# Which products of a decoder block begin with a matmul whose columns go in blocks

## The chip, the core and the metric

The kernel runs on one core of one Trainium2 chip. The metric is device time in microseconds (us) of one execution of the whole program. Weights and activations are float32 in HBM; most matmuls take them as float32r, the form in which TensorE multiplies a float32 operand.

## What is computed

One layer of a hybrid decoder trunk on 512 tokens of width 1024, with a memory of 256 tokens. Cut to what matters here:

```python
h = rmsnorm(x) * g
proj = h @ w_in                       # 9216 columns: B, C, v | u, ug | q | three gates
y_a = (B * conv3(C * v)) @ w_a_out
u   = conv31(u * sigmoid(ug)) + bias
y_b = silu(layernorm(u)) @ w_b_out
k, vm = split(rmsnorm(mem) @ w_kv)
s   = (q @ k.T) / 16                  # 4 heads of 256, 256 memory tokens
y_c = (softmax(s) @ vm) @ w_att_out
x   = x + (g0 * y_a + g1 * y_b + g2 * y_c) @ w_o
h2  = rmsnorm(x) * g2
gt, up = split(conv3(h2 @ w_up))      # 2 x 2816 columns
x   = x + (silu(gt) * up) @ w_down
out = rmsnorm(x) * g3
```

## The kernel before

**Products in three parts.** A float32 operand is split into a high part (rounded to float32r) and a low part (the rest). A product then takes three matmuls: high by high, high by low, low by high. ScalarE writes the high part of a weight unit (`whi`, line 665), VectorE the low part (`wlo`, line 669). A unit has 128 x 1024 elements; there are four pairs of such buffers, so unit n+4 waits until TensorE is done with unit n.

**Quads.** The wide projections (`w_in`, `w_up`, and `w_b_out`) are done in quads: two column groups of 256 by two halves of the depth by two halves of the tokens, with seven block products instead of eight, numbered 1 to 7. Sums of weight blocks are formed by DMAs that add (issued by GpSimd, line 790), sums of activations once by VectorE. A quad product, for instance `(("up", 1), 4)`, is one call of `multiply`: 2 x 4 x 3 = 24 matmuls of 128 x 128 weights by 256 columns, all recorded at line 845. The stationary operand is the weight part, the moving operand a form of the activations (`ft4h` is the high part of form t4). Results add up in PSUM banks (`bank`); ScalarE copies and VectorE adds them out (jobs `r1` to `r7`).

**The other products.** `product` (lines 616 to 618) makes three matmuls of a stationary activation by moving weights or keys: values `V`, scores `s`, the weighted values `o`, the output projection `wo`, and the down projection `pd`. The `merge` products are at lines 1654 to 1656. Of these, scores have 256 columns and the last group of `pd` (key `g`) partly so; the others have 512. The scores of a head are two calls with 12 matmuls each (`("s", h, 0)` and `("s", h, 1)`); after the softmax, its probabilities are transposed by four 128 x 128 transposes a call (`("pt", h, 0)`, `("pt", h, 1)`, line 1350).

**A matmul in blocks.** In some products the first matmul alone reads its moving columns, and writes its PSUM columns, in another order: the columns are cut into runs of `run` elements, first all even runs, then all odd ones. Column and place stay together, so the result is the same. It is done by a view:

```python
t.rearrange("p (b two r) -> p two b r", two=2, r=run)
```

Before the change the first matmul of a quad product has runs of 16 where the product just before it in TensorE's order has long rows (`V`, `o`, `merge`, `pd`, most of `wo`) or is a mean or a sum of squares; in the up projection, number 7 of quads 3 to 10 has runs of 64, 16 or 8 in turn. Each call of `scores` begins with a matmul in runs of 16 too.

**Order.** TensorE's order is written out: `seq`, a list of keys put together by loops over the quads and then changed by the pairs in `MOVES` (a key, and the key that it is put ahead of). A planner then places the work of ScalarE, VectorE, SyncE and GpSimd by costs and due times, and every engine issues in the order so found. The form of a matmul's columns is in no cost, so it moves nothing in any of these orders.

Of the kernel before, what the change touches and what calls it, by code (L numbers as in the profile page):

```python
# [58 lines left out]
WO_WHOLE = "f"  # L59
# [87 lines left out]
}  # L147

MOVES = [
    (("v", "squares"), (("gate", 1, 1), 6)),  # L150
    (("v", "rows"), ("merge", 0, 3, 0)),
# [341 lines left out]
def hybrid_block_kernel(  # L493
# [19 lines left out]
    nc = tc.nc  # L513
# [31 lines left out]
    def make(key, dtype=F32):  # L545

        ring, i = jobs.place[key]
        label = "_".join(str(k) for k in key) if isinstance(key, tuple) else key
        if ring == "ps":
            t = psum.tile([P, SEQ], F32, tag=f"ps{i}", name=name(str(key[0])))  # L550
        elif ring == "wf":
            t = wts.tile([P, 1024], F32, tag=f"wf{i}", name=name("wf"), bufs=1)
        else:
            t = places[ring].tile([P, 1024], dtype, tag=f"{ring}{i}", name=name(str(key[0])))
        tiles[key] = t
        return t

    def two(key):

        return tiles[key].rearrange("p (c n) -> p c n", c=2)  # L560
# [4 lines left out]
    def halves(key):  # L565

        return tiles[key].rearrange("p (c n) -> p c n", c=2)
# [32 lines left out]
    def par(key, i):  # L600
        return pk[:, cols[key] + i : cols[key] + i + 1]
# [4 lines left out]
    nc.scalar.dma_start(out=pk[:, :N_GAINS], in_=packed[:, :N_GAINS])  # L606
    nc.scalar.copy(mean_w, mean_col.broadcast_to([P, P]))

    def in_blocks(t, run):
        return t.rearrange("p (b two r) -> p two b r", two=2, r=run)  # L610

    def product(ps, w_hi, w_lo, s_hi, s_lo, start, stop, again=False, run=None):


        to, col = (ps, w_hi) if run is None else (in_blocks(ps, run), in_blocks(w_hi, run))
        nc.tensor.matmul(to, s_hi, col, start=start, stop=False, skip_group_check=again)  # L616
        nc.tensor.matmul(ps, s_hi, w_lo, start=False, stop=False, skip_group_check=again)  # L617
        nc.tensor.matmul(ps, s_lo, w_hi, start=False, stop=stop, skip_group_check=again)  # L618

# [7 lines left out]
    seq, pe_jobs, unit_uses, unit_at = [], {}, [], {}  # L627
# [192 lines left out]

    def long_rows(key):

        return key[0] in ("V", "o", "merge", "pd") or key[0] == "wo" and key[1] not in WO_WHOLE or key[1] in ("mean", "squares")

    def multiply(q, f, act):
        if f in (1, 2, 5):
            make(("bank", q, BANK_OF[f]))
        ps = halves(("bank", q, BANK_OF[f]))
        (w_hi, w_lo), (hi, lo) = w_units.pop((q, f)), form[act, OPERAND[f]]
        run = None  # L830
        if long_rows(seq[seq.index((q, f)) - 1]):
            run = 16
        elif q[0] == "up" and f == 7 and q[1] > 2:
            run = (64, 16, 8)[q[1] % 3]

        for c in range(2):
            at = slice(c * P, (c + 1) * P)
            for k in range(4):
                first = f in (1, 2, 5) and k == 0 and c == 0
                again = not (f in (1, 2, 5) and c == 0)  # L840
                for n, (w, a) in enumerate(((w_hi, hi), (w_hi, lo), (w_lo, hi))):
                    to, col = ps[:, c, :], a[k]
                    if run is not None and (c, k, n) == (0, 0, 0):
                        to, col = in_blocks(to, run), in_blocks(col, run)
                    nc.tensor.matmul(  # L845
                        to, w[:, k, at], col, start=first and n == 0,
                        stop=k == 3 and n == 2, skip_group_check=again,
                    )

    def multiply_job(q, f, act, unit=True):  # L850
        bank = ("bank", q, BANK_OF[f])
        after = [("wl", (q, f))]
        if (act, OPERAND[f]) in form_ready:
            after += form_ready[act, OPERAND[f]]
        else:
            after.append(("fl", act, OPERAND[f]))
        after += {6: [("r1", q)], 7: [("r6", q)], 4: [("r7", q)], 3: [("r5", q)]}.get(f, [])
        pe((q, f), 24 * MM_QUAD, lambda: multiply(q, f, act), after,
           take=[(bank, "ps")] if f in (1, 2, 5) else [], use=[] if f in (1, 2, 5) else [bank],
           unit=unit)  # L860
# [252 lines left out]
    def values_product(hp, kp, i):  # L1113
        w_hi, w_lo = w_units["V", hp, kp]
        first = kp == 0 and i == 0
        for c in range(MC):
            bank = ("bank", "V", hp, c)
            ps = make(bank) if first else tiles[bank]
            at, k = slice(c * P, (c + 1) * P), 2 * (kp % 2) + i
            product(  # L1120
                ps, w_hi[:, i, :], w_lo[:, i, :], tiles["mh", kp // 2][:, k, at],
                tiles["ml", kp // 2][:, k, at], first, kp == 3 and i == 1,
            )
# [101 lines left out]
    for i in range(2):  # L1225
        a, b = 2 * i, 2 * i + 1
# [106 lines left out]
    def scores(h, tp):  # L1333
        make(("bank", "s", h, tp))
        ps = halves(("bank", "s", h, tp))
        k = tiles["k", h].rearrange("p (s c n) -> p s c n", s=2, c=2)
        for i in range(2):
            t = 2 * tp + i
            at = slice(t * P, (t + 1) * P)
            for c in range(2):  # L1340
                product(
                    ps[:, i, :], k[:, 0, c, :], k[:, 1, c, :], two(("qh", h))[:, c, at],
                    two(("ql", h))[:, c, at], c == 0 and i == 0, c == 1, again=i > 0,
                    run=16 if (i, c) == (0, 0) else None,
                )

    def transposed(h, c):
# [6 lines left out]
    def weighted(h, d):  # L1354
        ps = make(("bank", "o", h, d))
        at = slice(h % 2 * 256 + d * P, h % 2 * 256 + (d + 1) * P)
        for c in range(MC):
            v_hi, v_lo = (two((s, h // 2))[:, c, at] for s in ("vh", "vl"))
            product(
                ps, two(("pth", h))[:, c, :], two(("ptl", h))[:, c, :], v_hi, v_lo,  # L1360
                c == 0, c == MC - 1,
            )

    def pe_scores(h):
        for tp in range(2):
            pe(("s", h, tp), 12 * MM_HALF, lambda tp=tp: scores(h, tp), [("kl", h), ("ql", h)],
               take=[(("bank", "s", h, tp), "ps")], use=[("k", h), ("qh", h), ("ql", h)],
               unit=False)
# [253 lines left out]
    for p in range(4):  # L1622
# [5 lines left out]
            lambda k, j, p=p: par("conv_a_w", k * KC + 2 * p + j), [("CV", p), ("ldp",)], ANY,  # L1628
# [40 lines left out]
    for br in (2, 0, 1):  # L1669
        for m in range(4):  # L1670
# [3 lines left out]
            gate = ("g", br, m)  # L1674
# [304 lines left out]
    for t in range(NT):  # L1979
# [8 lines left out]
        for i in range(2):  # L1988
            bank, r = ("bank", "tr", t, i), t // 2
# [37 lines left out]
    for q in range(QUADS):  # L2027
        up = ("up", q)
# [4 lines left out]
        for value, src, acc in ((0, ("gt", q), ("gtc", q)), (1, ("uu", q), ("upc", q))):  # L2033
            conv3_jobs(
                ("cf", q, value), src, acc,
                lambda k, j, q=q, v=value: par(
                    "conv_ffn_w", k * 2 * FC + v * FC + 2 * q + j),
# [253 lines left out]
    for u, ps in enumerate(PAIR_UNITS):  # L2291
        n = ps.stop - ps.start
        for p in "abe":
            i, j = {"a": (0, 0), "b": (1, 0), "e": (1, 1)}[p]
# [167 lines left out]

    for key, other in MOVES:
        seq.remove(key)
# [70 lines left out]
```

## Time and profile before

| what | us |
|---|---|
| median of 3 runs | 922.1 (920.11, 922.1, 924.8) |
| the profiled execution's own time | 922.01 |
| its span, first to last instruction | 920.2 |
| outside of the span | 1.8 |
| TensorE busy | 909.2 (99%) |
| VectorE busy | 849.7 (92%) |
| ScalarE busy | 685.9 (75%) |
| mean granted clock of TensorE | 0.998 |

A matmul's recorded duration (276 ns at line 845) is longer than the distance between two of them, since they overlap in the pipeline. What a matmul costs in a running stream is read from the distance of two starts, or from how many there are in a stretch. Weight loads (PEld) run beside the matmuls.

### The profile page before, as it was taken

What the parts mean: (1) busy time and instruction counts of PE and PEld (TensorE: products, weight loads), DVE (VectorE), ACT (ScalarE), POOL (GpSimd) and SP (SyncE); (2) the same over time, 40 slices, a digit from 0 to 9 for tenths busy, and PEclk for the clock granted to TensorE, in tenths of its full rate; (3) what the DMA queues carried; (4) which work ended last, traced back from release to release, by engine and by line L of the source; (5) the groups of instructions that cost most, each with busy time, mean ns of one, the idle gap of its engine ahead of it and who ended that gap; (6) DMA issues with size and microseconds to landing.
All of it is one profiled execution on the core that took longest, in us unless ns stands there. A gap on an engine that the chain in (4) does not pass through costs nothing.

```text
span 920.2 us, 17065 instructions
## 1 busy us (share of the span) xinstructions
PE 909.2 (99%) x6797; PEld 859.1 (93%) x6797; DVE 849.7 (92%) x969; ACT 685.9 (75%) x940; POOL 137.1 (15%) x164
## 2 busy tenths in 40 slices
PE   8999999999999999999999999999999999999997
PEld 8999999999989999999899997899999999988886
DVE  6997999999999998999888989898979899999977
ACT  8767989889997785979658964776667677765556
POOL 0021111100110221110111211121211121002300
PEclk9999999999999999999999999999999999999999
DMA  9999689564887999884969999999999698779972
GB/s 366 371 286 205 135 183 205 138 136 118 196 188 212 212 192 236 207 181 123 235 128 249 210 264 334 233 233 311 251 222 217 154 190 177 198 240 322 267 139 92
DMA packets 55520, 196.91 MB, mean 214 GB/s; under 512 B 6288, under 2 KB 6416, under 8 KB 55440
## 3 DMA queue, kind: packets, MB, share of 16 engines
q0 software_dynamic: 22608, 81.54, 49.3%
q1 hardware_dynamic: 32544, 114.02, 34.4%
q8 instruction: 53, 0.87, 0.4%
q10 hardware_dynamic: 288, 0.27, 0.1%
q14 instruction: 27, 0.22, 0.1%
HBM read 191.60 MB, written 4.19 MB: 213 GB/s over the span
## 4 chain that ended last, share of the span: by engine, by line
PE 91%; DVE 5%; DMA 2%; issue 1%; ACT 0%; SPq 0%; DVEq 0%; ACTq 0%
PE bank L845 61%; PE bank L618 6%; PE bank L616 6%; PE bank L617 6%; PE bank L1655 3%; PE bank L1656 3%; PE bank L1654 3%; DVE wlo L669 2%; PE bank L1107 1%; DMA wf<-in_w_v 1%; DMA ('up', 3)_967_7394<-in_w_up 1%; PE bank L1888 1%; DVE gtc L1610 1%; DVE zl L2224 0%; DMA wf<-in_w_kv 0%
## 5 line engine op out<-in xcount | busy, mean ns | idle before, releaser
L665 ACT CAST whi<-wf 128x1024 fp32r<-128x1024 f32 x200 | 208.1, 1045 | 86.2 <-PE bank L845 52.3
L669 DVE TENSOR_TENSOR wlo<-wf,whi 128x1024 fp32r<-128x1024 f32 x194 | 233.1, 1211 | 13.3 <-ACT whi L665 13.0
L1422 ACT ACTIVATE tp<-u,pk 128x511 f32<-128x511 f32 (+22 forms) x184 | 118.6, 703 | 2.3 <-DVE acc L1429 2.3
L1429 DVE TENSOR_TENSOR acc<-acc,tp 128x1022 f32<-128x1022 f32 (+22 forms) x92 | 109.1, 1188 | 6.5 <-ACT tp L1422 4.9
L790 POOL DMA_DIRECT2D wf<-in_w_in x46 | 41.6, 934 | 238.7 <-DVE wlo L669 216.4
L845 PE MATMUL bank<-ft4h,whi 128*128 128x256 f32 x248 | 68.7, 277 | 1.0 <-DVE uu L622 1.0
L845 PE MATMUL bank<-ft7h,whi 128*128 128x256 f32 x248 | 68.8, 277 | 0.7 <-ACT gt L887 0.7
L845 PE MATMUL bank<-fb11h,whi 128*128 128x256 f32 x248 | 68.8, 277 | 0.0
L845 PE MATMUL bank<-fb10h,whi 128*128 128x256 f32 x248 | 68.7, 277 | 0.0
L845 PE MATMUL bank<-ft6h,whi 128*128 128x256 f32 x248 | 68.7, 277 | 0.0
L845 PE MATMUL bank<-fb00l,whi 128*128 128x256 f32 x248 | 68.7, 277 | 0.0
L845 PE MATMUL bank<-fb00h,whi 128*128 128x256 f32 x248 | 68.7, 277 | 0.0
L845 PE MATMUL bank<-ft6l,whi 128*128 128x256 f32 x248 | 68.6, 277 | 0.0
L845 PE MATMUL bank<-ft4l,whi 128*128 128x256 f32 x248 | 68.6, 277 | 0.0
L845 PE MATMUL bank<-ft5h,whi 128*128 128x256 f32 x248 | 68.6, 277 | 0.0
L845 PE MATMUL bank<-ft4h,wlo 128*128 128x256 f32 x248 | 68.6, 277 | 0.0
L845 PE MATMUL bank<-ft7l,whi 128*128 128x256 f32 x248 | 68.6, 277 | 0.0
L845 PE MATMUL bank<-ft6h,wlo 128*128 128x256 f32 x248 | 68.6, 277 | 0.0
L845 PE MATMUL bank<-ft5l,whi 128*128 128x256 f32 x248 | 68.6, 277 | 0.0
L845 PE MATMUL bank<-fb11l,whi 128*128 128x256 f32 x248 | 68.6, 277 | 0.0
L845 PE MATMUL bank<-ft5h,wlo 128*128 128x256 f32 x248 | 68.6, 277 | 0.0
L845 PE MATMUL bank<-fb11h,wlo 128*128 128x256 f32 x248 | 68.6, 277 | 0.0
(413 smaller groups left out, 3168.5 us busy)
## 6 DMA issues: line engine op xcount, KB each, us to landing
wf<-in_w_in SPq DMA_DIRECT2D x50, 512.0 KB, 5.1
wf<-in_w_in POOLq DMA_DIRECT2D x46, 512.0 KB, 6.5
wf<-in_w_up POOLq DMA_DIRECT2D x33, 512.0 KB, 6.9
wf<-in_w_up SPq DMA_DIRECT2D x30, 512.0 KB, 6.5
wf<-in_w_down SPq DMA_DIRECT2D x15, 512.0 KB, 4.6
wf<-in_w_kv SPq DMA_DIRECT2D x8, 512.0 KB, 8.9
wf<-in_w_v SPq DMA_DIRECT2D x8, 512.0 KB, 8.1
wf<-in_w_att_out SPq DMA_DIRECT2D x8, 512.0 KB, 4.7
```

The source lines that it names most:

```text
L616: nc.tensor.matmul(to, s_hi, col, start=start, stop=False, skip_group_check=again)
L617: nc.tensor.matmul(ps, s_hi, w_lo, start=False, stop=False, skip_group_check=again)
L618: nc.tensor.matmul(ps, s_lo, w_hi, start=False, stop=stop, skip_group_check=again)
L665: nc.scalar.copy(parts[0], src())
L669: nc.vector.tensor_tensor(lo, src(), hi.bitcast(F32), op=ALU.subtract)
L790: nc.gpsimd.dma_start(out=tiles[key], in_=block(w, col[c], k), accum_op=ALU.add)
L845: nc.tensor.matmul(to, w[:, k, at], col, start=first and n == 0, stop=k == 3 and n == 2, skip_group_check=again,)
L1422: nc.scalar.activation(two(("tp", p, s))[:, j, s:], two(("u", p))[:, j, : SEQ - s], AF.Copy, scale=weight(j),)
L1429: nc.vector.tensor_tensor(a, a, two(("tp", p, s))[:, :, s:], op=ALU.add)
L1654: nc.tensor.matmul(ps, w_hi[:, i, at], hi, start=first, stop=False)
L1655: nc.tensor.matmul(ps, w_hi[:, i, at], lo, start=False, stop=False)
L1656: nc.tensor.matmul(ps, w_lo[:, i, at], hi, start=False, stop=last)
```

## The change

A set `FRESH` names nine quad products. A quad product now begins with a matmul in runs of 16 if it is in `FRESH`, or follows a transpose of probabilities (`pt`), beside the cases that there were. Five quad products follow a `pt`: `(("gate",2,0),2)`, `(("q",1),3)`, `(("gate",2,0),6)`, `(("gate",2,1),2)` and `(("gate",2,0),3)`. The scores lose their matmul in blocks: `product` no longer has a parameter for it. No instruction is added or taken away; what differs is the order of columns in the first matmul of 14 quad products and of the eight calls of `scores`.

```diff
+FRESH = {
+    (("glu", 1), 3), (("q", 1), 5), (("cv", 0), 1), (("cv", 2), 1), (("cv", 2), 2), (("bb", 1), 6),
+    (("gate", 0, 0), 3), (("up", 0), 7), (("up", 1), 4),
+}
...
-    def in_blocks(t, run):
-        return t.rearrange("p (b two r) -> p two b r", two=2, r=run)
-
-    def product(ps, w_hi, w_lo, s_hi, s_lo, start, stop, again=False, run=None):
-        to, col = (ps, w_hi) if run is None else (in_blocks(ps, run), in_blocks(w_hi, run))
-        nc.tensor.matmul(to, s_hi, col, start=start, stop=False, skip_group_check=again)
+    def product(ps, w_hi, w_lo, s_hi, s_lo, start, stop, again=False):
+        nc.tensor.matmul(ps, s_hi, w_hi, start=start, stop=False, skip_group_check=again)
         nc.tensor.matmul(ps, s_hi, w_lo, start=False, stop=False, skip_group_check=again)
         nc.tensor.matmul(ps, s_lo, w_hi, start=False, stop=stop, skip_group_check=again)
...
-        return key[0] in ("V", "o", "merge", "pd") or key[0] == "wo" and key[1] not in WO_WHOLE or key[1] in ("mean", "squares")
+        return key[0] in ("V", "o", "merge", "pd") or key[0] == "wo" and key[1] not in WO_WHOLE or key[1] in ("mean", "squares") or key[0] == "pt"
...
-        if long_rows(seq[seq.index((q, f)) - 1]):
+        if long_rows(seq[seq.index((q, f)) - 1]) or (q, f) in FRESH:
             run = 16
...
-                        to, col = in_blocks(to, run), in_blocks(col, run)
+                        to, col = blocks(to), blocks(col)
...
                     two(("ql", h))[:, c, at], c == 0 and i == 0, c == 1, again=i > 0,
-                    run=16 if (i, c) == (0, 0) else None,
                 )
```

More of the change, by code (lines that the diff above doesn't have):

```diff
@@ L834, in multiply, with blocks @@
             run = (64, 16, 8)[q[1] % 3]
+        def blocks(t):
+            return t.rearrange("p (b two r) -> p two b r", two=2, r=run)
         for c in range(2):
```

## The prediction

> **What bounds the kernel now.** I read the page first, for its chain of work that ended last, and then the chain in order of time.
>
> ```profile
> span 920.2 us, 17065 instructions
> ...
> PE 91%; DVE 5%; DMA 2%; issue 1%; ACT 0%; SPq 0%; DVEq 0%; ACTq 0%
> ```
>
> TensorE makes 91% of the chain. So the time is mostly the number of matmuls times the distance between two of them, and a change that only reorders columns inside a matmul can act through that distance alone. The chain in order of time shows how even the distance is.
>
> ```profile
> 177.89 2.73 PE bank L845 x24
> 180.62 0.44 PE bank L1350 x4
> 181.06 2.83 PE bank L845 x24
> ...
> 210.10 2.83 PE bank L845 x24
> ...
> 290.12 146.90 PE bank L845 x1296
> ...
> 636.99 151.73 PE bank L845 x1320
> 788.76 0.50 DVE wlo L669
> ...
> 827.87 0.50 PE bank L618
> ```
>
> Columns are start, us, and what. Between 290 and 437 us 1296 quad matmuls take 146.90 us: 0.1134 us each, 2.72 us for a quad of 24. The same rate would bring 1320 of them through in 149.6 us, yet the piece from 636.99 takes 151.73, so 2.1 us too long, with no wait in it. Two single quads that follow transposes (181.06 and 210.10) show the same on a small scale: 2.83 us against 2.73 for their neighbour at 177.89. To find where the 2.1 us lie I asked for stretches, with line 845 alone.
>
> ```profile
> 640.00:680.00 40.00, 40.00 (x342) 40.00 (x341) 1.00 1.04 260
> 690.00:700.00 10.00, 10.00 (x91) 10.00 (x90) 1.00 1.00 272
> 700.00:740.00 40.00, 40.00 (x355) 40.00 (x354) 1.00 0.79 162
> ```
>
> Columns: the stretch and its length, matmul busy time and count, weight loads likewise, granted clock, DMA share, GB/s. A matmul is recorded for 0.28 us, so a stretch of 40 us counts those that started in 40.28 us: 40.28/342 = 0.1178 us against 40.28/355 = 0.1135. Busy time is full and the clock is 1.00 in both. So TensorE has two rates for the same work, 4% apart, and a train of quads keeps one for tens of us. Where the slow train begins and ends stands in the timeline.
>
> ```profile
> 636.99 0.35 PE L845 MATMUL bank<-ft4h,whi 128*128 128x256 f32 x1 [0.99 <-DVE uu L622]
> ```
>
> ```profile
> 683.00 0.28 PE L845 MATMUL bank<-ft4h,whi 128*128 128x256 f32 x1
> ...
> 685.12 0.28 PE L845 MATMUL bank<-ft7h,whi 128*128 128x256 f32 x1
> 685.24 0.28 PE L845 MATMUL bank<-ft7l,whi 128*128 128x256 f32 x1
> 685.36 0.28 PE L845 MATMUL bank<-ft7h,wlo 128*128 128x256 f32 x1
> 685.48 0.28 PE L845 MATMUL bank<-ft7h,whi 128*128 128x256 f32 x1
> ```
>
> It begins at 636.99, with the first matmul after a wait for VectorE; by the written order that is `(("up",1),4)`. It ends at 685.12, which is `(("up",4),7)`, the first quad after it that has a matmul in runs of 16: from 683.00 to 685.12 lie 18 distances of 0.1178, then three of 0.12, and from there on the quads run at 0.1134. The block in runs of 64 in `(("up",3),7)`, in the middle of that train, ended nothing. I read this as a phase of the pipeline: a wait or a transpose can leave TensorE in the slow one, it stays there as long as equal matmuls follow, and a matmul in runs of 16 throws it into the fast one.
>
> **The change, part by part.** *The guard at `(("up",1),4)`.* From 636.99 to 685.12 are 17 quads. The 16 after the first would run at 0.1134 instead of 0.1178: 16 x 24 x 0.0044 = 1.70 us. In the first quad itself, 21 distances gain 0.0044 (0.09 us) and the block costs 0.03 us, as priced next: 0.06 us won.
>
> *The eight other named quads.* Here the block goes into a train that is fast already in this execution, or, at `(("up",0),7)`, follows a wait after which the train was fast by itself. The nearest row is `(("up",7),7)`, which has runs of 16 and enters from a fast train.
>
> ```profile
> 744.99 0.28 PE L845 MATMUL bank<-ft7h,whi 128*128 128x256 f32 x1
> ...
> 747.74 0.28 PE L845 MATMUL bank<-fb00h,whi 128*128 128x256 f32 x1
> ```
>
> Its 24 matmuls take 2.75 us instead of 2.72: 0.03 us. Eight of them cost 0.24 us; the bounds are 0 and 0.3.
>
> *The five quads behind transposes.* The two slow ones (2.83) come to 2.73: 0.20 us won. The other three pay up to 0.03 each; I take 0.05. Together 0.15 us won.
>
> A rule speaks against all three. The Trainium skill (SBUF — State Buffer, section Door 1: The DMA port swizzle) says that a PSUM access pattern that is not contiguous slows matmuls significantly. If that meant a matmul of twice the time (an estimate of mine, for the page has no figure), six more blocked matmuls than before would cost 0.7 us and the sum below would be 921.0; the rows at 685.12, with distances of 0.12, speak against it for runs of 16.
>
> *The scores without a block.* All their 96 matmuls now have rows of 256 columns in plain order.
>
> ```profile
> 165.65 0.28 PE L616 MATMUL bank<-k,qh 128*128 128x256 f32 x1
> ...
> 168.51 0.29 PE L845 MATMUL bank<-fb00h,whi 128*128 128x256 f32 x1
> ```
>
> ```profile
> 911.25 0.28 PE L616 MATMUL bank<-whi,zh 128*128 128x256 f32 x1
> ...
> 913.64 0.28 PE L618 MATMUL bank<-whi,zl 128*128 128x256 f32 x1
> ```
>
> With the block, the 24 matmuls of a head take 2.86 us: 0.119 each, neither of the two rates of the quads. The nearest rows without it are the last of the down projection, made by the same helper with 256 columns: 20 distances in 2.39 us, 0.1195 each. At that price the scores stay as they are (+0.05 us for four heads); if they took the rate of the quads, 96 x 0.006 = 0.6 us would be won. I take 0, since those rows are the same helper and width. The five quads right behind scores have no block, before or after, and lie in fast trains now; if plain scores left them slow, 5 x 0.1 = 0.5 us would be lost. I take 0 here too.
>
> *Does the end move with TensorE?* The chain above leaves TensorE at 788.76 and runs over VectorE until 827.87, where TensorE takes over to the end. So the 1.70 us count only if VectorE gets there earlier as well.
>
> ```profile
> 637.00:700.00 63.00, 63.00 (x540) 63.00 (x541) 54.67 (x63) 42.68 (x53) 12.16 (x14) 1.00 0.99 253
> 788.00:828.00 40.00, 39.63 (x262) 35.73 (x261) 39.75 (x45) 27.83 (x35) 0.86 (x1) 1.00 0.71 221
> ```
>
> ```profile
> ACT whi L665 <- PE bank L845: 33.2, 31, 1.8
> ```
>
> (Stretches: TensorE, weight loads, VectorE, ScalarE, GpSimd, clock, DMA; then the waits from 637 to 832 us: total, times, longest.) VectorE is full from 788 to 828 (39.75 of 40 us), so it can't catch up there. But from 637 to 700 it has 63 - 54.67 = 8.3 us idle, and what it idles for is ScalarE's high parts, which wait 33.2 us in all for TensorE to give buffers back. These come 1.7 us earlier, so VectorE can be 1.7 us ahead by 700 and the rest shifts as a whole. What is late next, in the first quads after the wait, is the low part for `(("up",3),1)`.
>
> ```profile
> 649.29 1.22 DVE L669 TENSOR_TENSOR wlo<-('up', 3)_967_7394,whi 128x1024 fp32r<-128x1024 f32 x1
> ```
>
> ```profile
> 651.20 0.28 PE L845 MATMUL bank<-fb00h,whi 128*128 128x256 f32 x1
> ```
>
> It is done at 650.51, 0.69 us ahead of its quad; by then five quads have won 0.06 + 4 x 0.106 = 0.48 us. It holds by 0.2 us, and if it didn't, the difference alone would be lost.
>
> **The sum.** -1.70 - 0.06 + 0.24 - 0.15 = -1.67 us. Against the profiled execution's own 922.01 us (span 920.2 and 1.8 around it) that gives 920.3. Its time is that of the median, 922.1, so I let 920.3 stand for the median too. The fastest run shown, 920.11, is what this execution would be without its slow train. Within 0.5% (4.6 us) lies about what a measurement of this kernel can tell from no change.
>
> **Rivals.**
>
> *Given back at VectorE's stretch (14%).* If VectorE's full stretch from 788 to 828 does not move, TensorE comes 1.7 us early and waits at 827.87. For it: 39.75 of 40 us busy there. Against it: 8.3 idle us before 700, and waits that TensorE itself ends. Time: 920.3 + 1.7 = 922.0.
>
> *The rate is no matter of phase (6%).* The slow stretch also has the highest DMA share, 1.04 against 0.79, so the rate could come from transfers beside it, and the blocks would do nothing. Against it: at 690 to 700 us the share is 1.00 and 91 matmuls in 10.28 us make 0.113. Then only the blocks' price is left: 922.2. The Trainium skill (SBUF — State Buffer, section SBUF: two separate sides) says that TensorE has ports of its own and never waits for the others, and that transfers cannot slow it; by that rule this rival falls, but the two rates at one busy share and clock have no place in it either.
>
> *The blocks throw fast trains out of step (5%): slower than before.* A phase that a block can mend, a block could spoil. Seven named quads stand in running trains: from each to the next block or the next product of another shape are 15, 8, 4, 2, 15, 15 and 7 quads, 66 in all by the written order. Slow, they lose 66 x 0.106 = 7.0 us: 927.3 with the gain at 636.99, 929 without. It decides the sign from 16 such quads on. Against it: the train behind 744.99 went on fast, as did that behind 685.12; for it, that only one block of 16 in the trace enters from a fast train.
>
> *Blocks cost as the first rule has it (2%).* 921.0, as worked out.
>
> *More is won (5%).* The three runs spread from 920.11 to 924.8, 4.7 us. If that spread is slow trains at other waits, with the median in the next measurement nearer to the top, then the change, which guards nine places, takes more than 4.6 us off it.
>
> **How the numbers follow.** The forecast keeps 68%. Its own bounds: best, with free blocks and scores at the quads' rate, 922.0 - 1.7 - 0.1 - 0.2 - 0.6 = 919.4; worst, with 0.3 for the eight, 0.1 for the three, slow quads behind the scores and the 0.2 us at 651, 921.2. The range reaches over the given-back and no-phase rivals to 923.0, with a spread of 0.8 us for the median of a few runs, and down by half as much to 919.0. Out of it are the slower rival and the case of more won, and some scatter. Faster by over 0.5%: 0.05; slower: 0.05; within: 0.90.
>
> **What would show it.** Right: from the quad after TensorE's last wait near 637 on, stretches of 40 us with 355 matmuls instead of 342; the quads behind transposes all at 2.73 to 2.75; the piece of the chain that took 151.73 us at 150; its scores at 2.86 a head; no new wait of TensorE between 640 and 826, and the wait near 827 no longer than now. Wrong: 342 matmuls in 40 us anywhere behind a block of 16 (phase not mended, or spoilt); a wait near 827 longer by 1.7 us (given back); a distance far over 0.12 behind a blocked matmul (a dear block).

## The result and the profile after

The changed kernel takes 920.32 us (median of 21 runs, 920.01 to 920.69), against 921.89 us for the kernel before in the same measurement (21 runs, 919.95 to 924.80). The ratio is 0.9981, with a 95% interval of 0.9975 to 0.9988: 1.6 us less, inside the 0.5% that the prediction called "within", and on its figure of 920.3. The profiled execution took 920.21 us at a granted clock of 0.998; before it was 922.01 us at the same clock.

First the page of the kernel after: the span, and the chain of work that ended last, by engine.

```profile
span 918.4 us, 17060 instructions
...
PE 92%; DVE 4%; DMA 2%; issue 1%; ACT 1%; SPq 0%; DVEq 0%
```

The span is 1.8 us shorter and TensorE's share of the chain still over 90%: nothing took its place. The chain in order of time (start, us, what) has the pieces that the prediction spoke of. Line 845 of before is line 848 here, and line 1350 is 1352.

```profile
177.91 2.74 PE bank L848 x24
...
181.09 2.76 PE bank L848 x24
185.66 2.75 PE bank L848 x24
...
210.06 2.76 PE bank L848 x24
...
213.26 2.76 PE bank L848 x24
...
290.06 147.00 PE bank L848 x1296
...
637.03 149.95 PE bank L848 x1320
787.02 0.50 DVE wlo L669
...
826.14 0.50 PE bank L618
```

The piece that took 151.73 us takes 149.95. VectorE's stretch begins at 787.02 instead of 788.76, and TensorE takes the chain over at 826.14 instead of 827.87. The piece of 1296 matmuls, which was fast before, is 0.10 us longer; four of the newly blocked quads lie in it. The stretches, with line 848 alone (length, matmul busy time and count, weight loads likewise, granted clock, DMA share, GB/s):

```profile
640.00:680.00 40.00, 40.00 (x356) 40.00 (x355) 1.00 1.05 262
690.00:700.00 10.00, 10.00 (x91) 10.00 (x90) 1.00 0.90 251
700.00:740.00 40.00, 40.00 (x355) 40.00 (x355) 1.00 0.79 166
```

From 640 to 680 us 356 matmuls start where 342 did, at the same clock and a DMA share of 1.05 instead of 1.04.

### The profile page after: what moved, and what is told of

Same layout as the page of the kernel before. It is cut to its first block, busy times and chain, and to the rows that moved or that the text cites. A ratio compares the mean times of both kernels' runs of the same rounds, so it can differ in the third digit from the quotient of the medians.

```text
span 918.4 us, 17060 instructions
## 1 busy us (share of the span) xinstructions
PE 906.8 (99%) x6797; PEld 856.7 (93%) x6797; DVE 849.7 (93%) x969; ACT 686.1 (75%) x940; POOL 137.2 (15%) x164
## 4 chain that ended last, share of the span: by engine, by line
PE 92%; DVE 4%; DMA 2%; issue 1%; ACT 1%; SPq 0%; DVEq 0%
PE bank L848 61%; PE bank L618 6%; PE bank L616 6%; PE bank L617 6%; PE bank L1656 3%; PE bank L1658 3%; PE bank L1657 3%; DVE wlo L669 2%; PE bank L1110 1%; DMA y_sum<-in_w_down 1%; PE bank L1890 1%; DMA wf<-in_w_v 1%; DVE zl L2226 0%; ACT whi L665 0%; DVE gtc L1612 0%
## 5 line engine op out<-in xcount | busy, mean ns | idle before, releaser
L848 PE MATMUL bank<-fb10l,whi 128*128 128x256 f32 x248 | 68.5, 276 | 0.0
L848 PE MATMUL bank<-ft7h,wlo 128*128 128x256 f32 x248 | 68.5, 276 | 0.0
L848 PE MATMUL bank<-fb00h,wlo 128*128 128x256 f32 x248 | 68.5, 276 | 0.0
```

The costliest lines, as they stand in the source:

```text
L848: nc.tensor.matmul(to, w[:, k, at], col, start=first and n == 0, stop=k == 3 and n == 2, skip_group_check=again,)
```

## The experiments

**My theory** is that of the prediction: a wait, a transpose or a product of another shape can leave TensorE in a slow phase of equal matmuls, 0.1178 us apart instead of 0.1133, and a matmul in short runs ends it. The gain is then the train at `(("up", 1), 4)`, and the other eight names only cost. **The rivals:** the rate comes from the transfers beside it; the other blocks guard trains that are slow in some executions; the scores without their block are a part of the gain; the rate is set by something else, such as where the operands lie.

### One guard alone

The kernel before with one more blocked quad.

```diff
-        if long_rows(seq[seq.index((q, f)) - 1]):
+        if long_rows(seq[seq.index((q, f)) - 1]) or (q, f) == (("up", 1), 4):
```

> The kernel before with one thing added: (up,1),4 begins with a matmul in runs of 16. If the gain comes from ending the slow train at 637 us, the 17 quads from there take 1.76 us less, and no other group moves by more than 0.1: median about 920.2. If the named quads in running trains or the quads behind transposes make the gain, nearly all of it stays away: 921.8 to 922.0. Since slow trains at other places are not guarded, single times should still reach above 921.

Measured: 920.32 us (11 runs, 919.93 to 923.10), ratio to the kernel before 0.9985 (0.9976 to 0.9994). Its chain has the long piece at the fast rate:

```profile
637.14 149.94 PE bank L845 x1320
```

This one block gives the median of the whole change, 920.32 as well. What the other thirteen blocks and the scores do cancels, or is too small to see here. Two of the eleven runs lie above 921 us (921.30 and 923.10), as was expected of trains without a guard; that they were slow trains was not seen. In the profile the two slow quads behind transposes are still slow, and no other quad is.

### The change without that guard

```diff
-    (("gate", 0, 0), 3), (("up", 0), 7), (("up", 1), 4),
+    (("gate", 0, 0), 3), (("up", 0), 7),
```

> The changed kernel without its guard at (up,1),4. Phase theory: the train behind the wait near 637 us runs at 0.1178 us a matmul again until (up,4),7, and the median is 920.3 + 1.75 = 922.0 to 922.1. If the gain came from several places together: 920.6 to 921.5. If the rate at 640 to 680 us is a matter of transfers and fell for another reason: 920.3.

Measured: median 921.87 us, ratio 0.9994 (0.9985 to 1.0002). The eleven runs stand in two groups: five from 919.88 to 920.63, and six from 921.87 to 922.43, with nothing between. The profiled one, 920.63 us, fell in the lower group, and in it the train is fast without a block at its head:

```profile
637.42 149.96 PE bank L848 x1320
```

```profile
640.00:680.00 40.00, 40.00 (x355) 40.00 (x354) 1.00 1.05 258
```

Two things follow. The same stretch with the same transfers (share 1.05) runs 355 matmuls here and 342 in the profile of before (share 1.04), so the transfers are not what sets the rate. The Trainium skill (SBUF — State Buffer, section SBUF: two separate sides) says that TensorE waits for nobody at its ports; as to transfers, these two rows agree with it. And whether the train stays slow is most likely chance: the wait ahead of this quad is 0.99 us here as in the profile of before, and the quad behind it has no block in either. The traces also show how this one got away. From start to start, its matmuls behind the first two are 0.117, 0.118, 0.122, 0.118, 0.114 and 0.113 us apart: it began at the slow rate and left it within its first quad, after one longer distance. In the changed kernel, behind its block, they are 0.118, 0.117, 0.116, 0.114 and 0.113; in the kernel before they stay at 0.117 to 0.119. What made the one distance longer is not shown.

The word chance rests on the times. The two profiles are of kernels that differ in other blocks, the nearest 18 us ahead, and only one execution of this kernel has a profile. But its eleven runs stand in two groups, and the gap between them is about the 1.8 us that the piece is worth. That every run of the upper group had the slow train was not seen; before's profile, at 922.01, had it. Of the 89 runs of the kernel before in all comparisons, 12 lie under 920.6 us, and 4 of these 12 are among the seven of one comparison, whose median is 920.20.

### The change without the seven blocks in running trains

```diff
-FRESH = {
-    (("glu", 1), 3), (("q", 1), 5), (("cv", 0), 1), (("cv", 2), 1), (("cv", 2), 2), (("bb", 1), 6),
-    (("gate", 0, 0), 3), (("up", 0), 7), (("up", 1), 4),
-}
+FRESH = {(("up", 0), 7), (("up", 1), 4)}
```

> The changed kernel without the seven named quads that stand in running trains; (up,0),7, (up,1),4 and the quads behind transposes keep their blocks. If those seven only cost 0.027 us each, the median falls by 0.19 us to 920.1. If they catch slow trains that begin at random waits in other executions, the middle falls a little but the highest times rise, to 922 and more, while the changed kernel's 21 runs stay within 920.0 and 920.7.

Measured: 920.20 us (11 runs, 919.90 to 920.59), ratio 0.9980 (0.9971 to 0.9989). I ran it once more, beside the changed kernel itself, to see whether the seven guard anything.

> The changed kernel without its blocks at the seven quads inside running trains, once more, on one chip with the changed kernel itself. Theory (the seven cost 0.027 us each and guard nothing): 0.2 us under the changed kernel, 920.1 against 920.3, and no run near 922. Rival (a train that is fast in the profiled run is slow in some other, and the seven end it there): a tail of runs 1 to 2 us up that the changed kernel doesn't have.

> The changed kernel as it is, beside the one without the seven. Theory: 920.3, all runs within 0.5 of it, 0.2 over the kernel without the seven. Rival (the seven guard): no tail here, and one there; or, if the tail of the kernel with blocks in the scores had nothing to do with the scores, a tail here too.

Measured: without the seven 920.02 us (11 runs, 919.69 to 920.36), with them 920.37 us (11 runs, 919.96 to 922.07). The piece of 1296 matmuls, first without the seven (both runs), then with them:

```profile
290.56 146.90 PE bank L845 x1296
```

```profile
289.81 146.90 PE bank L845 x1296
```

```profile
290.21 147.00 PE bank L848 x1296
```

The four blocks in this piece cost 0.10 us, 0.025 each; quad by quad, each of the seven goes from 2.720 to 2.746 or 2.747 us, 0.19 us in all. The medians differ by 0.35, more than that; the rest I can't assign. (The first medians of the two, 920.20 and 920.32, are 0.12 apart, but come from different measurements.) The rival of a guard falls as far as these runs go: the 22 runs without the seven stay under 920.6, while two of the eleven with them reach 921.0 and 922.07. So the tail is not one that the seven prevent. The kernel without the seven is the best version that I ran: by 0.19 us where the traces show the cause, by 0.35 in the medians measured side by side.

### The scores with their block again

```diff
+                    run=16 if (i, c) == (0, 0) else None,
```

> The changed kernel with the scores' matmul in blocks put back, as before. The trace after shows a head's 24 score matmuls at 1.421 + 1.440 us against 1.435 + 1.426 before, so the sum of a head is the same and the median stays at 920.3, within 0.1. If the block in the scores did something for the quads behind them, those would move by 0.1 us each, 0.5 us in all.

Measured: 920.37 us, ratio 0.9990 (0.9980 to 1.0000). Eight of the eleven runs lie from 919.99 to 920.83; three are at 921.80, 922.24 and 924.67. A head's two calls take 1.434 + 1.426 us with the block and 1.421 + 1.440 without, the same sum. In the changed kernel, the first score of a head and the first matmul behind its 24 are:

```profile
165.67 0.28 PE L616 MATMUL bank<-k,qh 128*128 128x256 f32 x1
...
168.53 0.29 PE L848 MATMUL bank<-fb00h,whi 128*128 128x256 f32 x1
```

That is 2.86 us a head, as before, so the scores are no part of the gain. The three high times I can't explain. The changed kernel, which has no such block, showed two in its second measurement and none in its first, so they don't speak for or against the scores.

### No blocks at all

```diff
-        if long_rows(seq[seq.index((q, f)) - 1]) or (q, f) in FRESH:
-            run = 16
-        elif q[0] == "up" and f == 7 and q[1] > 2:
-            run = (64, 16, 8)[q[1] % 3]
```

> The changed kernel with no quad product in blocks at all. If a product of another shape, a transpose or a wait leaves the quads behind it in the slow phase until a block ends it, every such train runs at 0.1178 us a matmul: with nearly all of the 217 quads slow, 217 x 0.107 = 23 us more, 940 or over. If most trains come into the fast phase by themselves, as those behind scores and the one behind 619 us do in the trace before, only a few stay slow: 920 to 925. If blocks do nothing, 920.0, as 34 of them cost up to 0.03 us each.

Measured: 933.28 us (4 runs, 929.66 to 935.46), ratio 1.0124 (1.0090 to 1.0159) to the kernel before. From its chain, and its stretches with the quads' line alone:

```profile
291.16 152.64 PE bank L844 x1296
```

```profile
345.00:385.00 40.00, 40.00 (x342) 40.00 (x342) 1.00 0.86 209
...
735.00:775.00 40.00, 40.00 (x342) 40.00 (x342) 1.00 0.77 157
```

In the profiled execution (935.37 us) 152 of the 217 quads run slow, none in the changed kernel: 152 x 0.107 = 16.3 us lost, less what 36 blocks cost, at most 0.027 each. Summed from the first matmul of each quad to the next matmul behind it, the 217 take 609.69 us instead of 594.06, 15.63 more; the two profiled times differ by 15.16. So the slow quads account for the difference, to within 0.5 us. The slow rate stands here at DMA shares of 0.77 and 0.86, which is the second proof against the transfers. The trains behind the 512-column products `o`, `merge` and `pd` are slow, those behind scores fast: the five quads right behind scores take 2.74 us, as with the scores' block. But not every product of 512 columns has slow quads behind it. Those behind `V` run fast without their blocks, and so does every quad up to 180 us.

### One block of each length

All blocks gone but three, each in the middle of a slow train.

```diff
+        run = {(("cv", 1), 4): 64, (("cv", 2), 2): 16, (("up", 5), 7): 8}.get((q, f))
```

> The changed kernel with no block at any quad but three, one of each length, each in the middle of a train that ran slow when no quad had a block: runs of 64 at (("cv",1),4), near 316 us; runs of 16 at (("cv",2),2), near 339; runs of 8 at (("up",5),7), near 727. Theory (a phase, which a matmul in short runs ends): the train goes on slow behind the runs of 64, 342 matmuls in 40 us; behind the runs of 16 it goes on at the fast rate, 355 in 40 us, until the merge at about 443: 37 quads x 0.107 = 4.0 us. What runs of 8 do is open: if they end it too, another 30 quads x 0.107 = 3.2 us by the next product of another shape at about 812. So about 929 without and 926 with it, against 933.3 with no block. Rival (the rate is set where a train begins, and a block inside it changes nothing): 342 in 40 us on both sides of all three, and 930 to 935.

Measured: 928.19 us in one run. The stretches lie behind the runs of 64 (the first, 16 us long), behind the runs of 16 (the second), ahead of and behind the runs of 8 (the last two):

```profile
320.00:336.00 16.00, 16.00 (x138) 16.00 (x137) 1.00 0.90 192
345.00:385.00 40.00, 40.00 (x355) 40.00 (x354) 1.00 0.90 215
660.00:700.00 40.00, 40.00 (x342) 40.00 (x341) 1.00 0.96 226
735.00:775.00 40.00, 40.00 (x355) 40.00 (x354) 1.00 0.80 164
```

With the 0.28 us that a matmul is recorded, 16.28/138 = 0.1180 us behind the runs of 64: they end nothing. Runs of 16 and of 8 both end the slow train within their own quad, and behind each the train is fast until the next product of another shape. The blocked quad itself falls from 2.826 to 2.738 us with 16 and to 2.737 with 8. The length that ends nothing also costs nothing: in the fast trains of the changed kernel, a quad that begins with runs of 64 takes 2.720 us, as one without a block, with runs of 8 2.733 and with runs of 16 2.747. Whether the order of the columns ends the train, or any delay as small as that, was not tested. That a matmul in short runs ends a slow train is shown here inside one execution, with two blocks that end it and one that doesn't. The expected 926 was missed by 2.2 us, most of it because the kernel without blocks, from which I took off, was put at its median of 933.3: the traced executions are 935.37 and 928.19, and their difference, 7.18, is the 4.0 + 3.2 that the two blocks were to win. In this execution the two quads `(("up", 0), 1)` and `(("up", 0), 2)` ran slow, in the other they ran fast, with no block at either in both: chance once more, as it seems.

### Other places for the moving operands

Before the activations' forms (the moving operands of the quads) the kernel sets aside 192 bytes a partition, so that they lie at a shifted address against the weights. Four runs change that figure and nothing else. The same figure moves the buffers of the memory's forms and of the parts of `w_o`, which lie in the same pool; the weights stay where they are.

```diff
-SHIFT = 192
+SHIFT = 256
```

> The changed kernel with the forms' buffers moved by another 64 bytes in every partition (SHIFT 256 for 192); nothing else differs. In the kernel before, matmuls with 256 columns run at 0.1133 or 0.1178 us where the moving operand lies 192 bytes off the weights (modulo 512), and at 0.1195 where it lies 0 off (scores, the end of pd). If the rate hangs on that offset, quads take another rate than 0.1133 and 0.1178; at 0.1195 it would be 5208 x 0.0062 = 32 us more, 952. If the two rates are a phase of TensorE alone, the offset does nothing: quads at 0.1133, 920.3.

> The changed kernel with SHIFT 64 for 192: the moving operand of quads 64 bytes off the weights (modulo 512). If the rate hangs on the offset, quads lie nearer to the 0.1195 us of offset 0 and the time rises by up to 32 us; if it is a phase of TensorE alone, 0.1133 and 920.3.

> The changed kernel with SHIFT 128. Measured so far: offsets 64 and 192 have two rates (0.1133 and 0.1178 us), offsets 0 and 256 have one, 0.120. If the rates repeat every 256 bytes, 128 is the place farthest from 0, between the two with two rates: either the fast rate alone (0.1133, at most 920.3, and no slow train left to guard against), or two rates again (920 to 940 by which one the trains take). If they repeat every 128 bytes, 128 is like 0: 0.120 and 953.

> The changed kernel with SHIFT 160, between 128 and 192. If offsets from 64 to 192 all have the two rates, the quads show 0.1133 and 0.1178 and nothing else, 920 to 940. If 128 is fast alone, 160 should be at 0.1133 for more of its trains than 192 without blocks is; with blocks 920.3 or less.

Measured: 953.53 us at 256 (one run), 941.09 at 64 (one run), 948.12 at 128 (4 runs, 947.91 to 948.33; ratio 1.0283, 1.0266 to 1.0301), 948.43 at 160 (one run). Stretches of the quads' line at 256, 64, 128 and 160 bytes:

```profile
320.00:360.00 40.00, 40.00 (x336) 40.00 (x335) 1.00 0.87 191
```

```profile
320.00:360.00 40.00, 40.00 (x342) 40.00 (x342) 1.00 0.86 192
```

```profile
320.00:360.00 40.00, 40.00 (x339) 40.00 (x338) 1.00 0.87 191
```

```profile
320.00:360.00 40.00, 40.00 (x336) 40.00 (x336) 1.00 0.84 188
```

40.28/336 = 0.1199 us at 256 and at 160, 0.1178 at 64, 0.1188 at 128, each in the stretch shown. Elsewhere the rate moves with the quad at 128 (0.1183 to 0.1202) and at 160 (0.1171 to 0.1200). So at 128 neither outcome came that was expected, and 160 is not like 192. These four kernels have all the 36 blocked quads of the changed one, yet no quad of theirs runs at 0.1133, except 17 of 217 at a shift of 64. Summed as above, the 217 quads take 33.4 us more than in the changed kernel at 256, 20.6 at 64, 27.4 at 128 and 27.5 at 160, which is the whole of what the kernels lose, to within 0.8 us. So where the moving operands lie decides which rates there are at all, and at 192 the blocks only choose between two of them. At 64 they mostly don't manage even that, which I did not follow up. The section of the Trainium skill cited above, by which TensorE waits for nobody at its ports, names no such effect. Here 33 us lie between 256 and 192 bytes, with the same instructions, the same transfers and a granted clock of 0.998 in both. Whether it is the distance from the weights or the place itself that counts, and which resource it touches, these runs do not show, since the weights were never moved.

## Why the prediction was right

*The guard at `(("up", 1), 4)`, -1.70 and -0.06.* Right. The 16 quads behind it go from 2.827 to 2.720 us each, 1.71 in all, and the quad itself from 2.901 to 2.814, 0.09. The chain's piece says the same, 151.73 - 149.95 = 1.78. The kernel with this guard alone and the change without it show it from both sides.

*The eight other names, +0.24.* Nearly right: seven cost 0.027 each, +0.19 by quads, and `(("up", 0), 7)` behind its wait costs nothing (2.843 to 2.836). The bounds were 0 and 0.3.

*The quads behind transposes, -0.15.* The right direction, the size a little off. The prediction let the two slow ones come from 2.83 to 2.73; by the chain they stand at 2.76, since they pay for their block; so the sign asked for, 2.73 to 2.75 at all five, was missed by 0.01 at three of them. These two were slow in all four profiles in which they have no block, so here the slow rate does not look like chance. The other three, 2.73, 2.75 and 2.74 before, are at 2.74, 2.75 and 2.76. The five pieces sum to -0.07 - 0.07 + 0.01 + 0.00 + 0.02 = -0.11.

*The scores, 0.* Right, by the 2.86 us a head on both sides. Plain scores left no quad behind them slow, in the changed kernel or with no block at all.

*The end moves with TensorE.* Right, and this was the step that carried the rival of 14%. The waits from 637 to 832 us (total, times, longest) and the stretch ahead of VectorE's full one (TensorE, weight loads, VectorE, ScalarE, GpSimd, clock, DMA), after:

```profile
PE bank L848 <- DVE uu L622: 1.0, 1, 1.0
PE bank L618 <- DVE zl L2226: 0.4, 1, 0.4
```

```profile
ACT whi L665 <- PE bank L848: 31.8, 30, 1.7
```

```profile
637.00:700.00 63.00, 62.97 (x555) 63.00 (x556) 56.30 (x64) 44.50 (x56) 12.20 (x14) 1.00 1.00 255
788.00:828.00 40.00, 39.63 (x253) 35.44 (x253) 39.76 (x45) 26.95 (x34) 0.68 (x1) 1.00 0.71 221
```

VectorE does 1.63 us more between 637 and 700 (56.30 against 54.67), and ScalarE's high parts wait 1.4 us less for TensorE. VectorE enters its full stretch 1.74 us earlier, by what TensorE won, and TensorE's last wait for it is 0.37 us long as before, only 1.73 us earlier. The low part for `(("up", 3), 1)`, for which the prediction left 0.2 us, came in time too:

```profile
649.14 1.22 DVE L669 TENSOR_TENSOR wlo<-('up', 3)_967_7394,whi 128x1024 fp32r<-128x1024 f32 x1
```

```profile
650.73 0.28 PE L848 MATMUL bank<-fb00h,whi 128*128 128x256 f32 x1
```

It is done at 650.36, 0.37 us ahead.

*The sum, -1.67 to 920.3.* The terms as measured make -1.78 + 0.19 - 0.01 - 0.11 = -1.71; the profiled times differ by 1.80, and the rest of 0.09 lies ahead of the first quad (0.03) and behind the last (0.06). The terms missed by up to 0.06 in both directions, so that the sum came out within 0.04 of its working is in part luck. *The rivals:* given back, no; transfers, no; fast trains thrown out of step, no (no quad of the changed kernel is slow); more won, no. The dear block of the Trainium skill's page on SBUF (section Door 1: The DMA port swizzle, as the prediction cites it) has 0.025 us against it here, for runs of 16.

*What the prediction did not see* is that the slow train at 637 is, by the times, a matter of chance. It took the profiled execution for the median one. That held because most runs of the kernel before lie in the upper group, though not all: a profile that fell on one of the 12 low runs would most likely have shown no slow train at 637, and against a median of 920.20, as in the one comparison, there would have been nothing to gain. That part of the hit was luck. The nine names were drawn as guards at nine places; by these runs one of them guards something.

## What to carry to other kernels

Compare the count of equal matmuls in equal stretches of a trace, not only busy time and clock: here two rates, 4% apart, stood behind the same "busy 40.00 of 40.00, clock 1.00", and behind one wait it looks like chance which of them a train kept. So look at the spread of many runs too, for groups with a gap between them. Put the reordering where a train was seen slow, and one block for each train; a block of 16 in a train that is fast cost 0.027 us and brought nothing. Before that, try the place of the operands: it moved this kernel by up to 33 us, and all its blocks together by 13.

## What was not expected of the hardware

The distance of two matmuls in a running train depends on where the moving operands lie in a partition, with the weights left in place: 0.1133 or 0.1178 us at a shift of 192, nearly always 0.1178 at 64, and in the stretches shown 0.1188 at 128 and 0.1199 at 160 and 256. A matmul with its columns in runs of 16 or 8 ends the slow rate at 192, one in runs of 64 doesn't. And behind one wait, ahead of the same instruction, a train kept the slow rate in some profiles and left it within a quad in another, without a block. What decides that, and what the two rates are inside TensorE, stays open.
